# The inverse scale of a weight group on ScalarE, as a product of powers of two

## The chip, the cores and the metric

The kernel runs on one core of a Trainium2 chip. The core has a matmul engine (TensorE, here PE, with its weight loads as PEld), VectorE (DVE), ScalarE (ACT), GpSimd (POOL) and SyncE (SP), and 16 DMA engines. Each engine runs its own list of instructions strictly in order and waits for the others by semaphores. The metric is the device time of one execution in microseconds; of several executions the median is given.

## The reference

A trunk of two layers on 512 tokens of 2048 features. Each layer normalises its input, multiplies it by one wide matrix `w_in`, and feeds three branches: a gated short convolution, a stick-breaking attention of 8 heads, and a gated linear attention (GLA) of 4 heads in chunks of 64 tokens. Each branch output is multiplied by a SiLU gate; the three are concatenated, multiplied by `w_out`, and added to the input.

```
h = _rmsnorm(x, norm_g)
proj = h @ w_in                       # 2048 -> 7696 columns, split into 13 parts
y_conv = _short_conv(cv_h, cv_b, cv_c, conv_w, conv_b) * silu(cv_g)
y_sb   = _stick_breaking(rms(q), rms(k), v) * silu(sb_g)
g      = log_sigmoid(gl_lr @ gla_w_up + gla_b_up) / 16
y_gla  = rms(_gla(gl_q, gl_k, gl_v, g)) * silu(gl_g)
return x + concat(y_conv, y_sb, y_gla) @ w_out
```

All of it is float32.

## The kernel before

**Float32 products from float16 halves.** Each operand of the wide products is split into a high and a low float16 half, and three matmuls (high by high, low by high, high by low) make one product. For that the values must lie in float16's range, so every weight group is multiplied by a power of two, and its result by the inverse power.

**Weight groups.** The two matrices are read in 76 groups of 256 columns, 38 for each layer (30 of `w_in`, 8 of `w_out`). While group i is multiplied, group i+2 is fetched (`fetch`, line 360: DMAs issued by POOL) and group i+1 is prepared. The preparation is hung into the matmul stream of group i by two hooks:

- `squares` (line 379, with 384 for a narrow extra part): ACT squares the whole group and sums each row. The output is thrown away (`junk`), the sums stay.
- `parts_of`: first `wscale`, then the splits. In `wscale` POOL adds the sums over the partitions (line 395), DVE adds the two halves into `m` (398), cuts its exponent out and halves it by integer operations (407: the result is the bit pattern of a number built from half the exponent), makes the scale `ws` from it (411: a constant minus the pattern) and the inverse scale `wu` (413: the pattern plus an offset held in a column, `inoff` for `w_in`, `outoff` for `w_out`). All of these are columns of 128x1. Then ACT makes the high half `wh` (450, 452 for the narrow part, 500) and DVE the low half `wl` (457, 459, 501).

`ws` is needed at once, by `wh` and `wl`. `wu` is read much later, when the group's products leave PSUM.

Some groups are *quick*: they are multiplied by a scheme of seven half-size products in place of eight, and need sums of quarters of the weights (lines 520 to 525) and sums of quarters of the tokens, which `sums_of` makes once for each layer (DVE line 719, with halves by ACT line 727; their tiles are `zw`, `g`, `s`). Quick products leave PSUM through ACT (793, 797) and DVE (794 and the lines behind it).

**What sets the order.** Nearly all instructions are put in order by a scheduler at build time, which runs a timeline of its own for each engine. The start is an exception: from line 107 to the `byhand.__exit__` line DVE and ACT keep among themselves the order in which the code is written. That written order ends with group 1's preparation and the last token copies: `wmax(1, 1)`, `wscale(1)`, `xhigh(3, 0)`, `xhigh(3, 1)`, `whi(1, 0)`, and so on. `xhigh` is an ACT copy of transposed tokens out of PSUM (577, out of psz_72 and psz_73 there), `xlow` the DVE subtraction that belongs to it (584). The token sums (719, 727) are not in the hand-ordered part, so the scheduler may put them in between.

**Then, in each layer,** come the GLA projections (828: two groups by token, the second with 16 extra columns), the other projections (686 to 688 plain, 778 and 781 quick), the GLA stage itself (1023 to 1150) woven into them, the attention in 128-query blocks, and the output projection. Line 1036 and 1133 are GLA's matmuls; 1121 makes the low half of its intra-chunk weights on DVE, and 1120 the high half on ACT.

Names in the order rows and the profile: `x_19` and `x_20` are the high and low tokens, `psp`, `psz` and `psm` are PSUM banks, `wh_74`, `wl_75`, `wh_76`, `wl_77` the two halves of group 1, `wh_110` to `wl_113` those of group 2. The profile leaves the numbers out. Lines from 414 on have a number lower by 1 in the changed kernel, from 1166 on lower by 2.

## Time and profile before

| | |
|---|---|
| median of 3 runs | 1655.18 us (1652.79 to 1658.44) |
| profiled execution, its own time | 1652.11 us |
| its span | 1650.3 us |
| PE busy | 1621.0 us (98%) |
| DVE busy | 1415.1 us (86%), 2377 instructions |
| ACT busy | 1185.3 us (72%), 1743 instructions |
| POOL busy | 270.0 us (16%) |

A row of a group of instructions reads: line, engine, operation, output and inputs with their shapes, count, then the busy time of all and the mean of one in ns, then the engine's idle time just before them and what ended it. A row of the timeline reads: start, length, engine, line, operation, and in brackets the idle time before it and the instruction that released it. The length of an instruction overlaps the start of the next on its engine; the distance of two starts is called its pitch here. A row of waits gives engine, tile and line that waited, the instruction that it waited for, the total in us, how often, and the longest.

### The profile page before, as it was taken

How to read it: one execution, taken by the hardware profiler on the slowest of the kernel's cores; microseconds unless marked ns; L12 is line 12 of the kernel's file. 1: busy time of each engine (PE TensorE's matmuls, PEld its weight loads, DVE VectorE, ACT ScalarE, POOL GpSimd, SP SyncE). 2: the span in 40 equal slices, each digit the busy share in tenths (PEclk: the TensorE clock that was granted, in tenths of full speed). 3: DMA queues.
4: the chain of work that ended last, by engine and by line, in shares of the span. 5: the costliest groups of instructions: out<-in, count | busy, mean ns of one | idle time of the engine just before them, and what ended most of it. 6: DMA issues, size and time to landing. Idle time of an engine off the chain costs nothing.

```text
span 1650.3 us, 41607 instructions
## 1 busy us (share of the span) xinstructions
PE 1621.0 (98%) x17914; PEld 1341.0 (81%) x17914; DVE 1415.1 (86%) x2377; ACT 1185.3 (72%) x1743; POOL 270.0 (16%) x298
## 2 busy tenths in 40 slices
PE   7999999999999999999999999999999999999999
PEld 5746668988999968789986467689898989668998
DVE  7977989969797979798689689898898989888893
ACT  8667787857777776756765687788786868666571
POOL 0121121111212121111112112112121212111110
PEclk9999999999999999999999999999999999999999
DMA  7144344496767686644543442635777766683441
GB/s 260 58 150 122 70 133 86 111 159 148 167 148 167 148 167 175 170 157 149 193 141 104 115 116 66 178 78 151 148 163 150 161 155 150 158 229 129 154 155 53
DMA packets 193913, 234.90 MB, mean 142 GB/s; under 512 B 90226, under 2 KB 154044, under 8 KB 193216
## 3 DMA queue, kind: packets, MB, share of 16 engines
q0 software_dynamic: 76992, 177.22, 39.9%
q1 hardware_dynamic: 107728, 45.56, 13.7%
q10 hardware_dynamic: 9008, 9.45, 1.8%
q8 instruction: 140, 2.29, 0.6%
q14 instruction: 45, 0.37, 0.1%
HBM read 179.65 MB, written 14.68 MB: 118 GB/s over the span
## 4 chain that ended last, share of the span: by engine, by line
PE 40%; DVE 5%; ACT 3%; DMA 1%; issue 1%; POOL 0%; DVEq 0%; ACTq 0%; POOLq 0%
PE psp L781 11%; PE psp L778 7%; PE psp L828 5%; PE psp L697 3%; PE psp L698 3%; PE psp L699 3%; PE psp L686 3%; PE psp L687 3%; PE psp L688 2%; DVE wl L501 1%; ACT junk L379 1%; ACT wh L500 1%; DVE za L1265 1%; PE psm L1289 1%; DMA st<-in_w_in_dram 1%
## 5 line engine op out<-in xcount | busy, mean ns | idle before, releaser
L500 ACT ACTIVATE wh<-st,ws 128x1024 f16<-128x1024 f32 x252 | 281.7, 1147 | 194.0 <-DVE st L520 96.7
L501 DVE SCALAR_TENSOR_TENSOR wl<-st,ws,wh 128x1024 f16<-128x1024 f32 x252 | 318.0, 1283 | 37.9 <-ACT wh L500 37.8
L379 ACT ACTIVATE junk<-st 128x2048 uint8<-128x2048 f32 x150 | 285.7, 1905 | 16.7 <-DMA st<-in_w_in_dram 8.5
L778 PE MATMUL psp<-s,wh 128*128 128x256 f16 x1152 | 195.6, 273 | 0.0
L778 PEld LDWEIGHTS <-wh 128*128 128x128 f16 x1728 | 168.3, 98 | 22.4 <-issue 2.1
L781 PE MATMUL psp<-wh,s 128*128 128x128 f16 x2048 | 176.7, 219 | 0.0
L697 PE MATMUL psp<-wh,m 128*128 128x256 f16 x640 | 174.5, 273 | 0.0
L698 PE MATMUL psp<-wl,m 128*128 128x256 f16 x640 | 174.5, 273 | 0.0
L699 PE MATMUL psp<-wh,m 128*128 128x256 f16 x640 | 174.5, 273 | 0.0
L781 PE MATMUL psp<-wl,s 128*128 128x128 f16 x1024 | 173.2, 219 | 0.0
L781 PEld LDWEIGHTS <-s 128*128 128x128 f16 x3072 | 172.9, 98 | 0.0
L457 DVE SCALAR_TENSOR_TENSOR wl<-st,ws,wh 128x2048 f16<-128x2048 f32 x68 | 158.9, 2347 | 14.7 <-ACT wh L450 14.7
L450 ACT ACTIVATE wh<-st,ws 128x2048 f16<-128x2048 f32 x66 | 130.7, 1998 | 41.8 <-DVE ws L411 22.8
L360 POOL DMA_DIRECT2D st<-in_w_in_dram x114 | 102.7, 905 | 344.3 <-DVE w7l L501 119.9
L778 PE MATMUL psp<-s,wl 128*128 128x256 f16 x576 | 156.7, 273 | 0.0
L395 POOL PARTITION_ALL_REDUCE wgm<-wm x75 | 54.3, 724 | 489.9 <-ACT junk L379 477.2
L781 PEld LDWEIGHTS <-m 128*128 128x128 f16 x2304 | 131.1, 98 | 2.2 <-issue 1.6
L382 POOL DMA_DIRECT2D st<-st x34 | 53.8, 1584 | 276.5 <-ACT junk L379 236.1
L778 PEld LDWEIGHTS <-wl 128*128 128x128 f16 x864 | 84.5, 98 | 16.0 <-issue 6.0
L781 PE MATMUL psp<-wh,m 128*128 128x128 f16 x1024 | 91.5, 219 | 0.3 <-DVE raw L794 0.3
L781 PE MATMUL psp<-wl,m 128*128 128x128 f16 x512 | 87.5, 219 | 0.0
L688 PEld LDWEIGHTS <-wl 128*128 128x128 f16 x448 | 43.8, 98 | 53.7 <-DVE wl L457 2.3
(442 smaller groups left out, 4203.0 us busy)
## 6 DMA issues: line engine op xcount, KB each, us to landing
st<-in_w_in_dram POOLq DMA_DIRECT2D x114, 1024.0 KB, 8.2
st<-in_w_out_dram POOLq DMA_DIRECT2D x32, 1024.0 KB, 8.4
st<-st POOLq DMA_DIRECT2D x34, 512.0 KB, 7.0
st<-in_w_in_dram SPq DMA_DIRECT2D x6, 1024.0 KB, 11.8
mixd<-g POOLq DMA_DIRECT2D x20, 256.0 KB, 6.9
x<-in_x_dram SPq DMA_DIRECT2D x4, 1024.0 KB, 5.1
qT<-in_x_dram ACTq DMA_DIRECT2D x8, 512.0 KB, 6.2
qT<-xs ACTq DMA_DIRECT2D x8, 512.0 KB, 3.9
```

What stands on the lines that cost most here:

```text
L360: queue.dma_start(s_, src[l, h * HK * P:(h + 1) * HK * P, c0:c0 + GW].rearrange("(k p) n -> p k n", p=P), max_dma_last_dim=1024)
L379: sq = S.activation(junk(HK * GW).rearrange("p (k n) -> p k n", k=part.shape[1]), part, AF.Square, accum_out=peak[i][:, h:h + 1])
L450: hi = S.activation(wh[:, :, :GW], staged[i][h], AF.Copy, scale=scales[i])
L457: V.scalar_tensor_tensor(wl[:, :, :GW], staged[i][h], scales[i], wh[:, :, :GW], ALU.mult, ALU.subtract)
L500: hi = S.activation(h_, b, AF.Copy, scale=sc)
L501: V.scalar_tensor_tensor(l_, b, sc, h_, ALU.mult, ALU.subtract)
L697: T.matmul(o, ah[:, t, k, :], wh[:, kk, :n], start=st_, stop=False, skip_group_check=True)
L698: T.matmul(o, ah[:, t, k, :], wl[:, kk, :n], start=False, stop=False, skip_group_check=True)
L699: return T.matmul(o, al[:, t, k, :], wh[:, kk, :n], start=False, stop=en, skip_group_check=True)
L778: mm = T.matmul(o, w[q_][:, kk, :], a[p_][:, :, kk, :], start=st_, stop=en, skip_group_check=True)
L781: mm = T.matmul(o[:, t * P:(t + 1) * P], a[p_][:, t, kk, :], w[q_][:, kk, :], start=st_, stop=en, skip_group_check=True)
L828: mm = T.matmul(o[:, :n], a_[:, t, k, :], w[k // HK][part][:, k % HK, :n], start=i == 0 and k == 0, stop=i == 2 and k == KT - 1)
```

## The change

The inverse scale `wu` of a group is no longer made by DVE from bit patterns. ACT makes it as a float product: it copies the pattern of line 407, read as a float (a power of two), and multiplies it by a column that now holds a power of two in place of an exponent offset. The columns `inoff` and `outoff` are products in place of integer sums, as many as before. The sum on line 398 takes its second operand as a column and gets a lower bound of 2^-120, so that the product has a normal number to work on.

```
-        V.tensor_scalar(inoff[lift], xun.bitcast(I32), float((50 + lift - 127) << 23), None, ALU.add)
+        V.tensor_scalar(inoff[lift], xun, 2.0 ** (50 + lift), None, ALU.mult)
...
-            first = V.tensor_tensor(m, gm[:, 0:1], gm[:, 1:2], ALU.add)
+            first = V.tensor_scalar(m, gm[:, 0:1], gm[:, 1:2], 2.0 ** -120, ALU.add, ALU.max)
...
         u = sm(1, "wu", bufs=6)
-        V.tensor_scalar(u.bitcast(I32), m.bitcast(I32), (outoff[l] if src is w_out else inoff)[lift][:, l:l + 1],
-                        None, ALU.add)
+        S.activation(u, m, AF.Copy, scale=(outoff[l] if src is w_out else inoff)[lift][:, l:l + 1])
...
-                V.tensor_scalar(outoff[l][lift][:, l:l + 1], pmx[:, 0:1].bitcast(I32), float((50 + lift - 127) << 23),
-                                None, ALU.add)
+                V.tensor_scalar(outoff[l][lift][:, l:l + 1], pmx[:, 0:1], 2.0 ** (50 + lift), None, ALU.mult)
```

The scheduler weighs the new instructions, so other instructions change places too. Three places follow. The first is ACT at the end of the hand-ordered part, where group 1 is prepared. Before:

```order
L384 ACTIVATE junk_67_359,wm_64_350<-kT_17_176 128x256
L577 ACTIVATE x_19_185<-psz_72_371 128x1024
L577 ACTIVATE x_19_185<-psz_73_381 128x1024
L727 ACTIVATE s_179_1275<-zw_181_1277 128x1024
L450 ACTIVATE wh_74_391<-st_16_173,ws_70_367 128x8x256
L452 ACTIVATE wh_74_391<-kT_17_176,ws_70_367 128x8x16
L917 ACTIVATE v_79_407<-psp_85_515 128x256
L379 ACTIVATE junk_104_684,wm_103_683<-st_82_410 128x2048
L450 ACTIVATE wh_76_399<-st_16_173,ws_70_367 128x8x256
L452 ACTIVATE wh_76_399<-kT_17_176,ws_70_367 128x8x16
```

The same place in the changed kernel:

```order
L384 ACTIVATE junk_67_359,wm_64_350<-kT_17_176 128x256
L726 ACTIVATE s_179_1275<-zw_181_1277 128x1024
L413 ACTIVATE wu_71_369<-wq_68_361,inoff0_156 128x1
L576 ACTIVATE x_19_185<-psz_72_371 128x1024
L576 ACTIVATE x_19_185<-psz_73_381 128x1024
L449 ACTIVATE wh_74_391<-st_16_173,ws_70_367 128x8x256
L451 ACTIVATE wh_74_391<-kT_17_176,ws_70_367 128x8x16
L916 ACTIVATE v_79_407<-psp_85_515 128x256
L726 ACTIVATE s_179_1275<-zw_182_1278 128x1024
L379 ACTIVATE junk_104_684,wm_103_683<-st_82_410 128x2048
L449 ACTIVATE wh_76_399<-st_16_173,ws_70_367 128x8x256
L451 ACTIVATE wh_76_399<-kT_17_176,ws_70_367 128x8x16
```

The new ACTIVATE stands ahead of the two token copies, as `wscale(1)` is written ahead of `xhigh(3, 0)`; the first token half (727, now 726) moved ahead of it, and a second one ahead of wh_76. On DVE the sum zw_181 that 726 reads has L302 and a copy L311 ahead of it, which stood behind it or later.

The second place is DVE where group 2's first low half, wl_111, is made. Before:

```order
L719 TENSOR_TENSOR s_179_1275<-zw_184_1296,s_179_1275 128x1024
L719 TENSOR_TENSOR zw_185_1297<-zw_185_1297,x_20_186 128x1024
L947 CAST qT_100_677<-lr_114_754 128x48
L947 CAST qT_100_677<-lr_116_813 128x48
L457 SCALAR_TENSOR_TENSOR wl_111_745<-st_82_410,ws_108_740,wh_110_744 128x8x256
L719 TENSOR_TENSOR g_186_1298<-zw_185_1297,g_186_1298 128x1024
L719 TENSOR_TENSOR zw_184_1296<-x_19_185,zw_185_1297 128x1024
```

And now:

```order
L718 TENSOR_TENSOR zw_185_1297<-zw_185_1297,x_20_186 128x1024
L948 TENSOR_TENSOR lr_114_754<-lr_114_754,qT_100_677 128x16
L948 TENSOR_TENSOR lr_116_813<-lr_116_813,qT_100_677 128x16
L917 SCALAR_TENSOR_TENSOR v_80_408<-psp_117_821,v_80_408 128x256
L718 TENSOR_TENSOR g_186_1298<-zw_185_1297,g_186_1298 128x1024
L718 TENSOR_TENSOR zw_184_1296<-x_19_185,zw_185_1297 128x1024
L946 CAST qT_100_677<-lr_114_754 128x48
L946 CAST qT_100_677<-lr_116_813 128x48
L456 SCALAR_TENSOR_TENSOR wl_111_745<-st_82_410,ws_108_740,wh_110_744 128x8x256
```

The sums g_186 and zw_184 moved from behind wl_111 to ahead of it.

The third place is DVE in layer 0's GLA stage, near the point where zw_319, a quick product, leaves PSUM. Before:

```order
L398 TENSOR_TENSOR wq_326_2745<-wgm_327_2746 128x1
L1110 SCALAR_TENSOR_TENSOR th_134_989<-zw_236_1718,th_134_989 128x256 x3
L407 TENSOR_SCALAR wq_326_2745<-wq_326_2745 128x1
L501 SCALAR_TENSOR_TENSOR w7l_314_2576<-st_216_1489,ws_305_2565,w7h_313_2575 128x1024
L411 TENSOR_SCALAR ws_328_2750<-wq_326_2745 128x1
L413 TENSOR_SCALAR wu_329_2752<-wq_326_2745,inoff1_158 128x1
L794 TENSOR_TENSOR zw_319_2685<-psp_321_2689,zw_319_2685 128x256
L1121 SCALAR_TENSOR_TENSOR za_256_2020<-psz_259_2023,za_256_2020 128x512
L1121 SCALAR_TENSOR_TENSOR e_258_2022<-psz_260_2042,e_258_2022 128x512
```

And now:

```order
L398 TENSOR_SCALAR wq_326_2745<-wgm_327_2746 128x1
L1109 SCALAR_TENSOR_TENSOR th_134_989<-zw_236_1718,th_134_989 128x256 x3
L1120 SCALAR_TENSOR_TENSOR za_256_2020<-psz_259_2023,za_256_2020 128x512
L407 TENSOR_SCALAR wq_326_2745<-wq_326_2745 128x1
L1120 SCALAR_TENSOR_TENSOR e_258_2022<-psz_260_2042,e_258_2022 128x512
L500 SCALAR_TENSOR_TENSOR w7l_314_2576<-st_216_1489,ws_305_2565,w7h_313_2575 128x1024
L793 TENSOR_TENSOR zw_319_2685<-psp_321_2689,zw_319_2685 128x256
L411 TENSOR_SCALAR ws_328_2750<-wq_326_2745 128x1
```

Two of GLA's low halves moved ahead of w7l and of zw_319, and L411 behind it; L413 is gone.

## The prediction

> **What bounds the kernel now.** I read the page's busy times first, then the engines by stretch, then what TensorE waited for.

> ```profile
> span 1650.3 us, 41607 instructions
> PE 1621.0 (98%) x17914; PEld 1341.0 (81%) x17914; DVE 1415.1 (86%) x2377; ACT 1185.3 (72%) x1743; POOL 270.0 (16%) x298
> ```

> TensorE (PE) is busy for 1621.0 of 1650.3 us, so 29.3 us is all that any edit beside the matmuls can win. The stretches show where those lie; after each start and end come the length and the busy time of PE, PEld, DVE, ACT and POOL.

> ```profile
> 0.00:41.30 41.30, 32.42 (x216) 24.20 (x217) 32.88 (x88) 33.67 (x46) 3.58 (x9) 0.96 0.78 260
> 41.30:82.50 41.20, 38.61 (x302) 29.29 (x300) 41.20 (x69) 27.04 (x32) 6.55 (x6) 1.00 0.20 58
> 82.50:165.00 82.50, 82.50 (x554) 45.87 (x553) 60.88 (x141) 57.03 (x72) 15.88 (x19) 1.00 0.47 136
> 165.00:206.30 41.30, 39.10 (x375) 26.66 (x374) 39.50 (x74) 32.97 (x58) 6.01 (x4) 1.00 0.32 70
> 330.00:412.00 82.00, 76.19 (x965) 70.12 (x963) 67.14 (x110) 56.02 (x91) 12.63 (x13) 1.00 0.82 155
> 1609.00:1650.30 41.30, 37.73 (x493) 35.29 (x490) 14.52 (x25) 7.70 (x8) 0.40 (x1) 0.99 0.17 53
> ```

> PE idles 8.9 us at the start, 2.6 at 41 to 82, none at 82 to 165, 2.2 at 165 to 206, 5.8 at 330 to 412 (where the DMA share is 0.82) and 3.6 in the tail, 23.1 together; the other 6.2 us lie in small pieces. Where PE never idles, work on VectorE (DVE) and ScalarE (ACT) is hidden. DVE is full (41.20 of 41.20) only at 41 to 82, so there its order decides. These are PE's waits that the edit could touch:

> ```profile
> PE psp L778 <- DVE zw L794: 3.9, 2, 2.0
> PE psp L828 <- ACT wh L441: 2.5, 1, 2.5
> PE psp L778 <- DVE w7l L501: 2.1, 2, 1.1
> PE psp L778 <- DVE g L794: 1.6, 1, 1.6
> PE psp L688 <- DVE wl L457: 1.3, 1, 1.3
> PE psp L828 <- ACT wh L450: 1.1, 1, 1.1
> PE psp L781 <- DVE raw L794: 1.0, 2, 0.7
> ```

> **The change, part by part. The tiny instructions.** These groups show those it touches, and the nearest to those it adds.

> ```profile
> L413 DVE TENSOR_SCALAR wu<-wq,inoff 128x1 int32<-128x1 int32 x60 | 12.4, 207 | 0.0
> L413 DVE TENSOR_SCALAR wu<-wq,outoff 128x1 int32<-128x1 int32 x16 | 3.3, 205 | 0.0
> L398 DVE TENSOR_TENSOR wq<-wgm 128x1 f32<-128x1 f32 x75 | 11.8, 157 | 24.7 <-POOL wgm L395 24.2
> L1343 DVE TENSOR_SCALAR gb<-wu 128x1 f32<-128x1 f32 x16 | 3.4, 213 | 0.0
> L205 ACT ACTIVATE xr<-xr 128x1 f32<-128x1 f32 x8 | 1.6, 203 | 0.2
> L202 ACT ACTIVATE xr<-ssq,epst 128x1 f32<-128x1 f32 x4 | 1.2, 289 | 0.1
> ```

> DVE loses 76 additions, 12.4 + 3.3 = 15.7 us. The 75 sums L398 turn from two tensors into a tensor with a column operand; L1343 is such an instruction, so each grows by about 213 - 157 = 56 ns, 4.2 us. DVE gains 11.5 us by duration. ACT gets 76 ACTIVATEs of 128x1: no row shows one with a column as scale, so it lies between L205 (203 ns, no column) and L202 (289 ns, a column as bias). I take L202, as the operand kind decides: 76 x 0.289 = 22 us, at least 15.4. Where ACT has slack neither figure is time: it is busy for 57.03 of 82.50 us where PE never idles. The six tiny instructions that make the offsets only change operation; I cost them at nothing, and the most they could lose is their number by 0.21 us, 1.2 us.

> [...]

> **The hand-ordered start.** In the first group the new ACTIVATE stands right ahead of the first wh on ACT, and PE waits for that wh 2.5 us (L828 <- ACT wh L441). Between 0.1 us (nothing but overlap) and 0.29 is added: I take **+0.2 us**.

> **The second group, 40 to 75 us: the largest term.** `wscale` of group 1 stands in the hand-written order ahead of the last two token copies (L577, psz_72 and psz_73). Before, ACT had nothing of `wscale` to do; now the inverse scale is on ACT, must wait for DVE's L407, and both copies and wh_74 stand behind it. ACT, DVE and PE now:

> ```profile
> 39.91 1.96 ACT L577 ACTIVATE x<-psz 128x1024 f16<-128x1024 f32 x2
> 43.42 1.06 ACT L727 ACTIVATE s<-zw 128x1024 f16<-128x1024 f32 x1 [1.55 <-DVE zw L719]
> 44.75 2.00 ACT L450 ACTIVATE wh<-st,ws 128x2048 f16<-128x2048 f32 x1 [0.27 <-DVE ws L411]
> 51.00 0.39 ACT L452 ACTIVATE wh<-kT,ws 128x128 f16<-128x128 f32 x1
> ...
> 42.17 1.22 DVE L719 TENSOR_TENSOR zw<-zw,x 128x1024 f32<-128x1024 f32 x1
> 43.30 0.15 DVE L407 TENSOR_SCALAR wq<-wq 128x1 int32<-128x1 int32 x1
> 44.63 0.20 DVE L413 TENSOR_SCALAR wu<-wq,inoff 128x1 int32<-128x1 int32 x1
> 44.75 1.21 DVE L584 TENSOR_TENSOR x<-psz,x 128x1024 f16<-128x1024 f32 x1
> 72.49 2.33 DVE L457 SCALAR_TENSOR_TENSOR wl<-st,ws,wh 128x2048 f16<-128x2048 f32 x1
> 74.75 1.20 DVE L719 TENSOR_TENSOR g<-zw,g 128x1024 f32<-128x1024 f32 x1
> 75.88 1.21 DVE L719 TENSOR_TENSOR zw<-x,zw 128x1024 f32<-128x1024 f16 x1
> ...
> 51.44 2.94 PE L828 MATMUL psp<-wh,x 128*128 128x272 f16 x24 [0.64 <-ACT wh L452]
> 74.88 0.39 PE L688 MATMUL psp<-x,wl 128*128 128x512 f16 x1 [1.31 <-DVE wl L457]
> ```

> The copies, 39.91 to 41.87, filled a hole ahead of L727, which waited for DVE. In the new order ACT waits for that sum first. It comes at about 43.9, since L302 and a copy L311 now stand ahead of it on DVE (before, the sum ran 42.17 to 43.39, so about 0.6 later). Then L727 to 45.1, the new ACTIVATE 0.2, two copies 1.96, and wh_74 starts at 47.3 instead of 44.75: 2.5 us late. wh_76 moves back further, since a second L727 is now ahead of it: its narrow part ends near 54.8 instead of 51.4, and PE resumes near 54.9 instead of 51.44, 3.5 us late. Later PE waited for DVE anyway: wl_111 began at 72.49, then came two sums, 74.75 and 75.88. In the new order these two are ahead of wl_111, 2 x 1.13 us, and DVE lost about 0.3 us more near 41, so wl_111 starts near 75.0 and PE gets it 2.5 us later than at 74.88. The two delays don't add: PE, 3.5 us late, gives 1.0 back out of its old wait of 1.31. Behind it PE has no idle time until 165 (82.50 of 82.50), so nothing there absorbs it: **+2.5 us**. Its bounds are 0 (the sums come earlier than this replay has them) and 3.5.

> **GLA stages.** PE waits twice for L794, 3.9 us. The first place is this:

> ```profile
> 193.81 1.28 DVE L501 SCALAR_TENSOR_TENSOR w7l<-st,ws,w7h 128x1024 f16<-128x1024 f32 x1
> 195.19 0.42 DVE L794 TENSOR_TENSOR zw<-psp,zw 128x256 f32<-128x256 f32 x1
> 195.52 0.68 DVE L1121 SCALAR_TENSOR_TENSOR za<-psz,za 128x512 f16<-128x512 f32 x1
> ...
> 195.66 0.27 PE L778 MATMUL psp<-x,wh 128*128 128x256 f16 x1 [2.03 <-DVE zw L794]
> ```

> In the new order L411 and L413 (0.06 + 0.12 us of pitch) no longer stand ahead of L794, but two L1121 of 0.60 us do, one of them ahead of w7l. PE, for its part, has 19 matmuls of the intra-chunk product and a pass over w7h and w7l ahead of the point where it waits, so it now waits for w7l, ready near 196.3; it fills about 1.2 us of the 2.8 us after 193.5 with work. 2.03 turns into about 1.6: **-0.4 us** (bounds -2.0, if PE arrives late from the first stretch and DVE doesn't, and +1.2, if both L1121 show). The twin in layer 1 has only one L1121 in place of L413, 0.60 for 0.12, and the old wait stays: **+0.5 us** (0 to 0.6).

> **Everywhere else** u stands mostly right ahead of its wh on ACT, where at the end of layer 0 PE waits 1.1 us for wh L450: **+0.1 us** (0.1 to 0.29). DVE's list is shorter by 0.12 us of pitch for each group (44.63 to 44.75 in the rows above) and longer by about 0.05 for L398. At the eight places where PE waits for DVE (3.9 + 2.1 + 1.6 + 1.3 + 1.0 = 9.9 us in the list) that is worth 8 x 0.07: **-0.5 us** (0 to -9.9, if all these waits went). Sum: 0.2 + 2.5 - 0.4 + 0.5 + 0.1 - 0.5 = **+2.4 us**. The profiled execution was 1652.11 us (span 1650.3 and 1.8 around it), so 1654.5; the median of the three runs lies 3.07 above it, so the forecast for the median is **1657.6 us**.

> **The rivals.** *Relief (faster).* DVE releases most of PE's waits, and it loses 76 x 0.12 = 9.1 us of pitch (44.63 to 44.75) and gains 75 x about 0.05 = 3.8: if the 5.3 us net reaches PE, the time is 1649.9. Against it: those waits lie at eight places, and only one or two tiny instructions stand ahead of each.

> *ACT's queue blocks (slower).* The mechanism of the second group repeats: an ACTIVATE that needs L407 stands at the head of an in-order queue, and DVE puts sums of 1.13 us between L398, L407 and L411. In layer 0's reshuffled GLA stretch some eleven such ACTIVATEs have other ACT work between them and their wh, which PE or DVE is fed by. It decides if PE has no lead over that work: six places that pass on 1.1 us make 6.6, on top of +2.4, so 1664.2. For it: DVE ended most waits of ACT, and wl then waits for wh.

> ```profile
> ACT wh L450 <- DVE ws L411: 22.8, 15, 5.3
> DVE wl L501 <- ACT wh L500: 37.8, 40, 5.4
> ```

> Against it: those 37.8 us cost PE next to nothing today, since hardly any wait of PE's list ends with them.

> *The slower engine for a small product (slower).* If each inverse scale were on the path, the difference of L202's 289 ns and L413's 207 would count 76 times, 6.2 us: 1661.4. [...] Against it: the list of PE's waits holds none that ends with L413, and where PE never idles ACT has 25 us of slack.

> *Nothing.* The delay at 75 is made up where PE waits for other things (the 5.8 us at 330 to 412 are largely transfers, DMA share 0.82, which would start no later), and 1655.2 stays. That the change doesn't do what it says I give no chance: the instruction order shows 76 ACTIVATEs in L413's place.

> **How the numbers follow.** About 0.3% (5.0 us) is what a measurement of this kernel can tell from no change. Forecast 0.55, nothing 0.18, blocked queue 0.17, slower engine 0.03, relief 0.07. The first two lie within 0.3% of 1655.18, the next two above 1660.1; relief at 1649.9 is just below 1650.2. So faster 0.07, same 0.73, slower 0.20. The range takes in half of the blocked case and stops short of the relief: 1652.0 to 1663.0. Forecast's own: 1655 to 1660.

> **What would show it.** L413 moves to ACT, 76 rows of 0.2 to 0.3 us; L398 near 0.21. In the stretch 41 to 82 PE idles about 5 us instead of 2.6, wh L452 released late near 54.8, wl_111 started near 75.0. PE's idle time at 165 to 206 falls from 2.2 to about 1.8, and at 82 to 165 it stays at zero. If PE idles newly at 82 to 165 or 206 to 330 behind ACT's wh, the queue blocks; if the waits for L794 and L501 vanish, it is relief. The forecast is wrong if 41 to 82 is unchanged.

## The result, and the profile after

The change is slower, and outside the range. Its median over four executions is 1670.31 us (1664.62 to 1679.99), against 1653.99 us (1648.19 to 1658.44) for four of the kernel before timed with it: a ratio of 1.0117, with a 95% interval from 1.0090 to 1.0144. The forecast was 1657.6 us and the range ended at 1663.0.

The unaltered change was timed twice more, beside the experiments. *again* had a median of 1667.16 us against 1651.12 (1.0114, 1.0083 to 1.0146), *again2* 1664.06 against 1653.09 (1.0063, 1.0039 to 1.0087). The lowest of all 14 executions is 1660.69 us, so every one is slower than the forecast, and they spread over 19 us. A steady loss and a loss that varies from execution to execution have to be told apart.

The page of the changed kernel (profiled execution 1679.99 us) begins so:

```profile
span 1678.2 us, 41610 instructions
PE 1631.6 (97%) x17914; PEld 1344.1 (80%) x17914; DVE 1410.7 (84%) x2301; ACT 1198.3 (71%) x1819; POOL 263.7 (16%) x298
```

DVE lost 76 instructions and ACT gained 76, as foreseen. PE has as many matmuls as before, but is busy for 10.6 us more: it ran at a lower clock in places (0.95 to 0.98 in three of the stretches below, 1.00 in the same stretches before). And it idles for 46.6 us instead of 29.3. The durations were right. These rows give, by line, the shortest, median and longest instruction in ns:

```profile
L413 ACT ACTIVATE wu<-wq,inoff x60: 278/294/351, 16.7 to 1477.3; 128x1 f32<-128x1 f32 x60
L413 ACT ACTIVATE wu<-wq,outoff x16: 278/294/297, 681.0 to 1642.4; 128x1 f32<-128x1 f32 x16
L398 DVE TENSOR_SCALAR wq<-wgm x75: 192/209/226, 42.9 to 1641.0; 128x1 f32<-128x1 f32 x75
```

The prediction had 289 ns for the first two and 213 for the third. So the price of the instructions is not where the time went. These are the stretches of the changed kernel, with the columns of the prediction's (after the five engines come the granted clock, the DMA share and GB/s):

```profile
0.00:41.30 41.30, 31.66 (x211) 23.62 (x212) 32.67 (x85) 32.64 (x45) 3.11 (x9) 0.96 0.78 260
41.30:82.50 41.20, 37.67 (x293) 28.82 (x292) 40.92 (x65) 28.84 (x35) 5.58 (x7) 0.96 0.17 54
82.50:165.00 82.50, 82.50 (x513) 45.56 (x511) 58.78 (x134) 53.20 (x72) 16.18 (x19) 1.00 0.44 130
206.30:330.00 123.70, 122.33 (x1398) 98.41 (x1396) 113.59 (x197) 100.01 (x154) 21.71 (x24) 1.00 0.43 114
330.00:412.00 82.00, 77.26 (x953) 70.29 (x951) 66.91 (x113) 56.72 (x100) 14.04 (x15) 0.98 0.79 148
1500.00:1600.00 100.00, 94.61 (x1003) 82.91 (x1002) 82.15 (x94) 60.94 (x64) 9.81 (x13) 0.95 0.46 149
```

At 41 to 82 PE now idles 3.5 us and the clock is 0.96; at 82 to 165 it idles not at all, as before. New are 1.4 us at 206 to 330 and 5.4 us at 1500 to 1600, where the clock falls to 0.95 as well; the kernel before idled at neither:

```profile
206.30:330.00 123.70, 123.70 (x1456) 101.26 (x1454) 116.03 (x211) 101.35 (x161) 23.79 (x26) 1.00 0.43 110
1500.00:1600.00 100.00, 100.00 (x1351) 94.74 (x1350) 87.42 (x101) 61.09 (x61) 11.64 (x15) 1.00 0.44 145
```

**Where the lag arises.** Every kernel here issues 16272 projection matmuls (tile `psp`). In short stretches neighbouring ones change places (at most 304 of them carry other tile names than in the kernel before, in the kernels of the table); everywhere else they come in the same order. So, away from these stretches, the start of the n-th can be compared between two traces; the difference is the lag behind the profiled execution of the kernel before. In us, at some places of the time before (the experiments in the right columns are explained below):

| time before | change | again | again2 | mix_other_queue | late_one | late_old2 |
|---|---|---|---|---|---|---|
| 41 | +0.8 | +1.3 | +1.4 | +1.8 | +1.1 | +1.4 |
| 150 | +3.0 | +3.6 | +3.6 | +4.0 | +1.0 | +1.2 |
| 210 | +2.4 | +2.9 | +3.0 | +3.3 | +2.7 | +0.8 |
| 350 | +4.7 | +5.2 | +5.3 | +5.6 | +2.9 | +0.9 |
| 380 | +4.6 | +5.5 | +5.3 | +0.3 | +3.0 | -4.9 |
| 900 | +8.6 | +6.2 | +6.1 | +1.8 | +3.7 | -2.5 |
| 1000 | +9.8 | +7.4 | +7.1 | +2.8 | +4.6 | -1.6 |
| 1150 | +12.1 | +8.1 | +7.7 | +3.4 | +6.9 | -1.8 |
| 1210 | +18.2 | +7.9 | +13.6 | +4.3 | +12.1 | -1.6 |
| 1480 | +18.8 | +8.2 | +14.5 | +4.5 | +12.0 | -0.5 |
| 1640 | +27.9 | +18.0 | +14.5 | +5.6 | +12.0 | -0.5 |

Three stretches hold the large jumps: 350 to 380 and 1150 to 1210, where the attention of a layer begins, and 1480 to 1500, where its last mixed outputs are loaded. A jump can be there in one execution of the changed kernel and missing in the next, and the kernel before had one itself at 350 to 380. *mix_other_queue* has the same change (one load moved to another queue), did not have that jump, and so gains 5.3 us there. Outside these stretches the three unaltered executions lose 12.8, 8.1 and 8.6 us and *mix_other_queue* 8.9 (the first one's 12.8 hold a slow load near 690, 3.0 us, and a stretch of half clock near 1020, 1.4 us; the second trace of that version, *mix_again*, loses 12.0, with 2 us between 1210 and 1480 that the others lack). That is the steady part, 8 to 9 us, and the prediction gave it 2.4. Of it 0.8 to 1.8 us are there at 41 us already. *null_swap* below, which leaves the inverse scale on DVE, has 1.0 us there too, so most of that is likely an early start of the one execution of the kernel before, and about 7 us are left behind 41 us. The rest, 15.1, 9.9, 5.9 and -3.3 us, is the varying part.

### The profile page after: what moved, and what is told of

The parts are those of the page before. It is cut to its first block, busy times and chain, and to the rows that moved or that the text cites. A ratio compares the mean times of both kernels' runs of the same rounds, so it can differ in the third digit from the quotient of the medians.

```text
span 1678.2 us, 41610 instructions
## 1 busy us (share of the span) xinstructions
PE 1631.6 (97%) x17914; PEld 1344.1 (80%) x17914; DVE 1410.7 (84%) x2301; ACT 1198.3 (71%) x1819; POOL 263.7 (16%) x298
## 3 DMA queue, kind: packets, MB, share of 16 engines
q8 instruction: 140, 2.29, 0.6%
## 4 chain that ended last, share of the span: by engine, by line
PE 21%; DVE 13%; ACT 8%; DMA 5%; issue 3%; POOL 0%; SPq 0%; DVEq 0%; ACTq 0%; POOLq 0%
PE psp L780 5%; PE psp L827 3%; DVE wl L500 2%; PE psp L698 2%; PE psp L696 2%; PE psp L697 2%; ACT junk L379 2%; ACT wh L499 2%; PE psp L777 2%; PE psp L685 2%; PE psp L686 2%; PE psp L687 1%; DMA m<-mixd 1%; DMA st<-in_w_in_dram 1%; DMA st<-st 1%
## 5 line engine op out<-in xcount | busy, mean ns | idle before, releaser
L500 DVE SCALAR_TENSOR_TENSOR wl<-st,ws,wh 128x1024 f16<-128x1024 f32 x252 | 317.5, 1280 | 46.2 <-ACT wh L499 46.1
L449 ACT ACTIVATE wh<-st,ws 128x2048 f16<-128x2048 f32 x66 | 130.6, 1994 | 30.7 <-PE psp L686 13.0
L395 POOL PARTITION_ALL_REDUCE wgm<-wm x75 | 48.6, 648 | 520.7 <-ACT junk L379 505.5
```

What stands on the lines that cost most here:

```text
L449: hi = S.activation(wh[:, :, :GW], staged[i][h], AF.Copy, scale=scales[i])
L500: V.scalar_tensor_tensor(l_, b, sc, h_, ALU.mult, ALU.subtract)
```

## The experiments

**The change once more: again.** No edit.

> The changed kernel unaltered, for a second trace. If its loss belongs to its order (ScalarE's queue in the second group, and waits for transfers late in each layer), the waits for the copied tokens near 44 us (about 2.6 us) and for the rescaled mix near 685 and 1507 us (2.5 and 5.1 us) come again and the ratio stays near 1.012. If the long transfers of the first trace (20 us to landing instead of 10) were a disturbance of that one execution, the waits near 1183 and 1507 us shrink to under 1 us, the granted clock is near 0.998, and the ratio falls to 1.006 to 1.008.

**And once more: again2.** No edit.

> The changed kernel once more, for more executions beside the three below on one chip. If slow transfers strike at random in some executions, its times fall in groups: about 1658 without any, about 1663 with one of 5 us, 1668 to 1680 with the late mix. If they belonged to this order, all would lie at 1664 and above, as the eight so far did.

Measured: 1.0114 and 1.0063, as above. What follows: the first timing was no accident, and the lags up to 350 agree within 0.6 us in all three. Of the waits that *again* was to show, those near 44 us (2.59) and near 1507 us (3.96 and 1.19) came again; the one near 685 did not. The six executions of *again2* fall into two groups 5 us apart, 1660.7 to 1661.9 and 1666.2 to 1666.9, as the expectation has it for transfers that are slow in some executions, but none comes near its 1658. What differs comes mostly from two of the three stretches, 1150 to 1210 (+6.1, -0.2, +5.9 us) and behind 1480 (+9.1, +9.8, 0.0).

**The second group's ACTIVATE moved behind the copies: late_one.** The change, but the ACTIVATE of group 1 alone is issued behind the two copies and behind `wh_74`.

```diff
-        S.activation(u, m, AF.Copy, scale=(outoff[l] if src is w_out else inoff)[lift][:, l:l + 1])
+        late[i] = (u, m, (outoff[l] if src is w_out else inoff)[lift][:, l:l + 1])
+        if i != 1:
+            unscale(i)
...
+    def unscale(i):
+        u, m, off = late.pop(i)
+        S.activation(u, m, AF.Copy, scale=off)
...
     whi(1, 0)
+    unscale(1)
```

> The change with one instruction moved: group 1's inverse scale is made behind the last two token copies and the first high half, not ahead of them. By ScalarE's queue the wait near 44 us (2.6 us) and the stretch of half clock near 48 us (3.4 us at half speed, 1.7 us) go, so it is 3 to 5 us faster than the change: a ratio 0.002 to 0.003 lower. If the second group is made up for later, or the loss lies elsewhere, it stays where the change is.

The timeline of the changed kernel shows what it is to undo (start, length, engine, line):

```profile
44.57 1.06 ACT L726 ACTIVATE s<-zw 128x1024 f16<-128x1024 f32 x1 [3.96 <-DVE zw L718]
45.53 0.28 ACT L413 ACTIVATE wu<-wq,inoff 128x1 f32<-128x1 f32 x1
45.72 1.92 ACT L576 ACTIVATE x<-psz 128x1024 f16<-128x1024 f32 x2
46.78 2.52 PE L827 MATMUL psp<-wh,x 128*128 128x256 f16 x16 [2.58 <-ACT x L576]
47.53 2.00 ACT L449 ACTIVATE wh<-st,ws 128x2048 f16<-128x2048 f32 x1
75.47 2.33 DVE L456 SCALAR_TENSOR_TENSOR wl<-st,ws,wh 128x2048 f16<-128x2048 f32 x1
77.86 0.39 PE L687 MATMUL psp<-x,wl 128*128 128x512 f16 x1 [0.58 <-DVE wl L456]
```

ACT stands idle for 3.96 us, then come the sum's half, the new ACTIVATE and the two copies, and PE waits 2.58 us for the first of the copies. In *late_one* (its lines 837, 465 and 697 are 827, 456 and 687 of the change) the same places read:

```profile
44.37 1.91 PE L837 MATMUL psp<-wh,x 128*128 128x256 f16 x16
47.38 2.24 PE L837 MATMUL psp<-wh,x 128*128 128x256 f16 x16 [1.10 <-DVE zun L191]
73.54 2.33 DVE L465 SCALAR_TENSOR_TENSOR wl<-st,ws,wh 128x2048 f16<-128x2048 f32 x1
75.92 0.39 PE L697 MATMUL psp<-x,wl 128*128 128x512 f16 x1 [1.66 <-DVE wl L465]
```

The wait of 2.58 us is gone, `wl_111` starts 1.93 us earlier, and PE has it at 75.92 instead of 77.86. From 41 to 150 us the lag of the change grows by 2.2 us, that of *late_one* not at all (1.1 and 1.0). The median is 1664.10 us, 3.06 below *again* on the same chip; its ratio of 1.0082 (1.0048 to 1.0115) overlaps the one of *again*, so the trace shows this step and the timing alone would not. What follows: the mechanism that the prediction gave the second group is there and worth 2.2 us, but it is only a part: *late_one* is still slower than the kernel before. Behind 150 us the two can't be compared step by step, since the scheduler gave *late_one* another order in layer 0's GLA stage too: there it has a wait of 2.29 us at 197, with half clock behind it (granted clock 0.96 from 165 to 206, 1.00 in the change), and none at 222 where the change has one.

**The halves alone: only_sum, old_sum.** *only_sum* is the kernel before with the new L398, *old_sum* the change with the old one.

```diff
-            first = V.tensor_tensor(m, gm[:, 0:1], gm[:, 1:2], ALU.add)
+            first = V.tensor_scalar(m, gm[:, 0:1], gm[:, 1:2], 2.0 ** -120, ALU.add, ALU.max)
```

> The kernel before with one of the changes alone: the sum of a group's two halves takes a column operand and a lower bound; the inverse scale stays an integer addition on VectorE. If the loss is ScalarE's queue (the new instruction ahead of the two token copies), this is within 0.2% of the kernel before. If the loss comes from the scheduler's reordering, which this edit sets off as well, it is as slow as the change, 1.008 to 1.014.

> The change with the old sum (two tensors, no lower bound), the inverse scale on ScalarE. If ScalarE's queue is the cause, as slow as the change, 1.008 to 1.014, and the second group waits about 2.6 us for the copied tokens. If the reordering by the longer sum is the cause, within 0.3% of the kernel before.

Measured: *only_sum* 1655.34 us, 1.0041 (1.0021 to 1.0060); *old_sum* 1650.89 us, 1.0016 (0.9992 to 1.0041). With the inverse scale on ACT and the old sum the time cannot be told from before in the median, though two of its ten executions took 1666 and 1668 us against 1649 to 1656 of the others. *old_sum* still waits 2.53 us for the copies near 47 us, so that wait does not make the change as slow as it is. By the middle of the intervals the smaller half, a sum longer by some 50 ns, costs more than the half that gives the change its name; the two intervals overlap, so this order of the two is not shown. Neither expectation of *only_sum* came: it is slower than before by more than 0.2%, and by half as much as the reordering alone was to cost. The middles of the two halves add up to 0.57%: near the lower one of the three results for the whole, and below the intervals of the other two.

**Two edits that change next to nothing: null_swap, dve_twice.** *null_swap* is the kernel before with the lines that make `ws` and `wu` exchanged. *dve_twice* is the kernel before with line 413 standing twice, so that DVE has 76 more of just the instructions that the change takes from it (the second overwrites the first with the same value).

```diff
-        sc = sm(1, "ws")
-        V.tensor_scalar(sc.bitcast(I32), m.bitcast(I32), -1.0, float((204 - lift) << 23), ALU.mult, ALU.add)
         u = sm(1, "wu", bufs=6)
         V.tensor_scalar(u.bitcast(I32), m.bitcast(I32), (outoff[l] if src is w_out else inoff)[lift][:, l:l + 1],
                         None, ALU.add)
+        sc = sm(1, "ws")
+        V.tensor_scalar(sc.bitcast(I32), m.bitcast(I32), -1.0, float((204 - lift) << 23), ALU.mult, ALU.add)
```

```diff
         V.tensor_scalar(u.bitcast(I32), m.bitcast(I32), (outoff[l] if src is w_out else inoff)[lift][:, l:l + 1],
                         None, ALU.add)
+        V.tensor_scalar(u.bitcast(I32), m.bitcast(I32), (outoff[l] if src is w_out else inoff)[lift][:, l:l + 1],
+                        None, ALU.add)
```

> The kernel before with the inverse scale emitted ahead of the scale on VectorE: the same 76 + 76 instructions, the wide scale 0.12 us later. If small changes of order cost what the change costs, this may lie anywhere between 0.997 and 1.010. If only real work counts, it is within 0.3% of the kernel before.

> The kernel before with the removed cost doubled: VectorE makes each inverse scale twice, 76 more instructions of 0.12 us, 9 us of VectorE. If VectorE's small instructions are on the path, 5 to 9 us slower, 1.003 to 1.006. If they are hidden and only order counts, the same as the kernel with the longer sum alone, whose order it nearly shares, 1.002 to 1.006 through the same places, or the same as before.

Measured: 1654.07 us, 1.0009 (0.9993 to 1.0025), and 1654.53 us, 1.0009 (0.9994 to 1.0025). What follows: 76 more instructions on DVE, 76 x 0.12 = 9.1 us of pitch, with the order that came with them, cost at most 0.25%, and 0.09% by the middle. That is a net figure: the trace of *dve_twice* gains 5.1 us of lag at 350 to 380, where its transfers lie apart (below), and loses elsewhere. In *null_swap* the scale `ws`, where nothing but the exchanged line stands between, starts 0.31 us behind line 407 in place of 0.18. That is more than the 0.05 us that the longer sum adds ahead of it, and the time stays within 0.25% of before. Together they speak against the length of the tiny instructions, taken away or added, as the source of a per cent. And not every new order costs: these two moved instructions too.

**Both at once: late_old, late_old2.** The old sum and the late ACTIVATE of group 1 together; the inverse scales stay on ACT. *late_old2* is the same kernel timed again on another chip, with the change beside it.

> Both edits that helped alone, together: the inverse scale on ScalarE with the old sum, and group 1's inverse scale behind the last token copies. If the second group's 3 us were not made up for in the kernel with the old sum, this is about 3 us faster than that one, 1648 us, a ratio of 0.998 to 0.999 to the kernel before. If every order stands for itself and gains don't add, anything from 1.000 to 1.008.

> The best version so far again, to tell its 0.16% from nothing: 0.997 to 0.9995 if it is really faster by the 3 us that the second group no longer loses and the 5 us that the transfers at the start of layer 0's attention cost the kernel before; 1.000 or more if the first result was luck.

Measured: 1648.71 us, 0.9984 (0.9967 to 1.0001), then 1648.62 us, 0.9975 (0.9958 to 0.9992). The second interval is below one: in that timing this version beats both kernels, the one before by a quarter of a per cent (the first interval just includes one). In its text it differs from the change in one DVE operand form and in the place of one ACTIVATE of 0.28 us, and the time differs by 15 us (1664.06 against 1648.62 on the same chip). What follows: the inverse scale on ACT costs nothing by itself. What costs is, as far as these runs go, the order that the whole program got with it. No run has the longer sum in an otherwise unchanged order; that its 50 ns are not the cause rests on *null_swap* and *dve_twice*.

One piece of that order can be seen where the attention of layer 0 begins. There `qT` is made by DMA transposes from SP's queue, while POOL fetches weights. In the kernel before:

```profile
333.25 9.73 SPq L1366 DMA_TRANSPOSE qT<-qp  x2
335.25 1.77 POOL L360 DMA_DIRECT2D st<-in_w_in_dram  x2 [3.91 <-DVE wl L457]
```

and in the view of the DMA issues of 325 to 362 us (KB each, median us to landing):

```profile
st<-in_w_in_dram POOLq DMA_DIRECT2D x4, 1024.0 KB, 12.4
st<-st POOLq DMA_DIRECT2D x1, 512.0 KB, 17.6
```

The same two views of *late_old2*, and its stretch of 330 to 412:

```profile
332.05 6.72 SPq L1374 DMA_TRANSPOSE qT<-qp  x2
338.86 1.76 POOL L360 DMA_DIRECT2D st<-in_w_in_dram  x2 [5.87 <-DVE wl L465]
```

```profile
st<-in_w_in_dram POOLq DMA_DIRECT2D x4, 1024.0 KB, 8.5
st<-st POOLq DMA_DIRECT2D x2, 512.0 KB, 8.3
330.00:412.00 82.00, 81.33 (x1068) 75.85 (x1066) 72.66 (x120) 63.95 (x113) 14.34 (x17) 1.00 0.72 155
```

Before, the fetch is issued 2.0 us behind the transposes, while they run; the fetches land after 12.4 us and the transposes take 9.73. In *late_old2* the fetch comes 6.8 us behind, when the transposes are done, the fetches land after 8.5, and PE idles 0.7 us in a stretch where it idled 5.8. The change has the distance of before:

```profile
337.94 9.78 SPq L1364 DMA_TRANSPOSE qT<-qp  x2
339.82 1.77 POOL L360 DMA_DIRECT2D st<-in_w_in_dram  x2 [3.92 <-DVE wl L456]
```

Eight profiled executions (before, *null_swap*, *late_one*, the change three times, and twice with the other queue for the mixed loads, below) have the fetch 1.9 to 2.1 us behind the transposes in both layers. Those are 16 places, and at 10 of them PE waited for `kT<-raw`, 2.6 us on average, with further waits behind. In the six others (*only_sum*, *old_sum*, *dve_twice* and the three with both edits) no weight fetch is issued while the transposes run, and of their 12 places one has such a wait, of 0.4 us. This association is shown; it was not tried by moving the transposes and nothing else. And the place of the fetch alone does not decide it. With the wait the two transposes of `qT` took 9.73 us (layer 0 before), 9.78 and 8.94 (both layers of the change), 9.31 (layer 0 of *again*) and 7.75 (layer 1 of *again2*). Without it, at the same distance, they took 5.46 in layer 1 of the kernel before and 4.94 in layer 0 of *mix_other_queue*, no longer than where they lie apart (6.72 in *late_old2*, 7.01 in *only_sum*). *mix_other_queue* in layer 0:

```profile
338.87 4.94 SPq L1364 DMA_TRANSPOSE qT<-qp  x2
340.75 1.77 POOL L360 DMA_DIRECT2D st<-in_w_in_dram  x2 [3.92 <-DVE wl L456]
```

The change itself had both in layer 1: the wait at first (transposes of 8.94 us) and in *again2* (7.75), and none in *again*. So, as far as these traces go, the order makes the loss possible, and something that no run here shows decides in which execution it comes. A loss that comes in some executions fits the spread: the kernel before took 1644.6 to 1664.6 us in 29 executions, *late_old2* 1647.2 to 1654.2 in twelve beside them (*late_old* had one of twelve at 1663.7).

**The mixed loads: mix_other_queue, mix_again, late_old_mix.** In the profiled executions of the change and of *again* PE waits near 1500 us for `m`, the mixed outputs that are loaded back for the output projection. DMA view, DVE and PE of the change:

```profile
m<-mixd SPq DMA_DIRECT2D x2, 256.0 KB, 20.6
1510.65 0.49 DVE L1172 TENSOR_SCALAR m<-m,ratio 128x1024 f16<-128x1024 f16 x1 [5.82 <-DMA m<-mixd]
1511.20 0.40 PE L698 MATMUL psp<-wh,m 128*128 128x256 f16 x1 [3.90 <-DVE m L1172]
```

Before, the same loads landed after 9.4 us:

```profile
m<-mixd SPq DMA_DIRECT2D x2, 256.0 KB, 9.4
```

The edit lets one half of these loads be issued by ACT's queue instead of SP's: on the change (*mix_other_queue*, and *mix_again* on another chip) and on the best version (*late_old_mix*).

```diff
-    order(nc.sync.dma_start(mix[i][:, :, ks, :], mixd[l]...), lastmm[0])
+    order((nc.scalar if i else nc.sync).dma_start(mix[i][:, :, ks, :], mixd[l]...), lastmm[0])
```

> The change, with the low half of the stored branch outputs fetched by ScalarE's DMA queue rather than SyncE's, where it stands behind the transposes. If PE's wait near 1500 us is this transfer, queued behind slow transposes, the wait for the rescaled mix (5.2 us and half clock after it, 10 us together) goes and the kernel is 4 to 10 us faster than the change, 1657 to 1663 us, with no execution over 1668. If all transfers are slow there whatever their queue, the wait stays at 4 us or more and the time at 1664 to 1680.

> The change with the low half of the stored branch outputs fetched by ScalarE's DMA queue, again, for more executions than four. If that transfer behind slow transposes is what makes the change's slowest executions, the median stays 4 to 8 us below the change's on this chip and no more than one in ten lies above 1668. If the four were luck, the median is within 2 us of the change's.

> The best version so far (old sum, group 1's inverse scale behind the copies) with the low half fetched by the other queue as well. If the queue takes away an execution like its 1663.68 and nothing else, the median stays at 1648 to 1650 and the highest under 1656. If ScalarE pays for issuing three transfers a layer, 1 to 2 us slower.

Measured: *mix_other_queue* 1662.53 us over four executions, 1.0076 (1.0049 to 1.0103); *mix_again* 1661.86 us over twelve, 1.0051 (1.0032 to 1.0070), 2.2 us below *again2* beside it, with intervals that overlap; *late_old_mix* 1651.42 us, 0.9982 (0.9963 to 1.0001), 2.8 us above *late_old2* beside it, with a highest execution of 1658.11: neither the median nor the highest that the expectation gave for the queue as the cause. The profiled execution of *mix_other_queue* had no wait near 1500. That of *mix_again* had one again, for another transfer:

```profile
PE psm L1287 <- DMA th<-za: 7.1, 2, 6.4
```

Inconclusive: of the 4 to 8 us expected of *mix_again* 2.2 came, two of its twelve executions lay above 1668, and SP's queue is not shown to be the cause. The late transfers strike some executions of several kernels (*old_sum* lost 16 us here in its profiled execution, *late_one* nothing with nearly the order of the change). Why some and not others stays open.

## Why the prediction was wrong

**The prices were right and did not matter.** 294 ns and 209 ns stood against 289 and 213. The forecast was argued correctly that far: the work on ACT is hidden, as *old_sum* and *late_old2* show.

**The second group: right mechanism, size nearly right.** The prediction had PE get `wl_111` 2.5 us late; it was 77.86 - 74.88 = 2.98 us in the first trace, but 0.8 of that was there at 41 us, ahead of the group. From 41 to 150 us the lag grows by 2.2 us in all four traces of the change's order in the table, +2.5 was forecast. `wl_111` started at 75.47 where 75.0 was forecast. The way there differed: PE waited at the copies themselves (2.58 us), not for `wh_76`. That wait had a consequence that no row of before announces. In *again*, this is the time right after it, with the clock as the third number from the end:

```profile
47.50:50.70 3.20, 3.20 (x16) 2.28 (x15) 3.20 (x7) 3.20 (x5) 0.00 (x0) 0.50 0.01 3
```

The granted clock is 0.50 there, in the trace of the change for 3.41 us (48.02 to 51.43). That costs 1.7 us of matmul time, but here not on top: PE arrived later at `wl_111`, and its old wait of 1.31 us shrank to 0.58, since DVE set the moment. PE's idle time at 41 to 82 rose to 3.5 us and not to the 5 of the prediction's sign, since part of the delay is slower matmuls and not idle time.

**The start: +0.2 not resolvable.** PE's wait for the first `wh` was 2.7 us in the change, but 1.3 in *again*, 1.6 in *again2* and 2.4 in *mix_other_queue*, against 2.5 before. It varies by more than the term.

**GLA, layer 0: the number was near, the wait was another, and the next wait was missed.** From 150 to 210 the lag falls by 0.6 to 0.8 us in all four; -0.4 was forecast. But PE does not wait for `w7l` there, as the replay had it. The scheduler moved GLA's own matmuls ahead on PE, and these wait 0.79 us for the second of the two low halves:

```profile
198.05 0.83 PE L1132 MATMUL psz<-th,v 128*128 128x128 f16 x12 [0.79 <-DVE e L1120]
```

So the nearness of the number is partly luck. (The replay also says that one of the two low halves stands ahead of `w7l`; in the order rows both do, and its 196.3 us for `w7l` counts both. `w7l` ended at 199.2 in a trace that was some 3 us late.) Then the lag rises by 2.3 us up to 350, in all four alike. Most of it, 1.5 us, is one place, some 25 us behind the one that the prediction replayed:

```profile
220.12 0.68 DVE L1147 TENSOR_TENSOR e<-e,e 128x512 f32<-128x512 f32 x1
220.72 1.00 DVE L1196 TENSOR_SCALAR kT<-zw,par 128x512 f32<-128x512 f32 x2
221.63 0.42 DVE L793 TENSOR_TENSOR qT<-psp,qT 128x256 f32<-128x256 f32 x1
222.10 0.27 PE L777 MATMUL psp<-x,wh 128*128 128x256 f16 x1 [1.37 <-DVE qT L793]
```

The kernel before, with lines higher by 1 or 2:

```profile
211.98 1.00 DVE L1198 TENSOR_SCALAR kT<-zw,par 128x512 f32<-128x512 f32 x2
216.14 0.42 DVE L794 TENSOR_TENSOR qT<-psp,qT 128x256 f32<-128x256 f32 x1
217.97 0.69 DVE L1148 TENSOR_TENSOR e<-e,e 128x512 f32<-128x512 f32 x1
```

DVE now does L1196 (once far ahead) and L1147 (once behind) right before the L793 that PE waits for, and PE has a wait of 1.37 us where it had none. So the stretch where "PE never idles" in the profile of before got a new bound by order alone.

**GLA, layer 1: +0.5 exactly, and again not all.** From 1000 to 1012 the lag rises by 0.5 us in *again*, *again2* and *mix_other_queue*. In the first trace it rises by 1.9, with a stretch of half clock behind the wait (0.50 for 3.41 us from 1020.82; why only there is not shown). But from 900 to 1000 all four lose 1.0 to 1.2 us that no term covered, and from 380 to 900 another 0.7 to 1.5 (4.1 in the first trace, where a slow load of `m` near 690 adds 3.0).

**The end of layer 0: +0.1.** The wait for `wh` L449 grew from 1.1 to 1.7 us, the lag rose by 0.6 at 822, and at 845 it was given back.

**Relief, -0.5: not seen.** No stretch shows it, and *dve_twice* points the same way: 9.1 us of DVE pitch more, with its order, cost 0.09%.

**The step that failed is "everywhere else".** The sum was made of the places that were looked at, and every other place was taken to keep its order but for 0.12 us of pitch. The places that were replayed came out near the forecast: 2.2, -0.6, 0.5 and 0.0 us behind 41 us, 2.1 together, where 2.7 was forecast. But the whole program was reordered, and the terms that nobody replayed (+2.3, +1.2, +0.7 us and more) came to about 5 us of the steady 7, where -0.5 was forecast. Also wrong was the clause, in the rival "nothing", that the transfers at 330 to 412 "would start no later" and were therefore no part of the matter: late transfers there, at 1150 to 1210 and near 1500 make the varying part, 5 to 10 us at a time. That the profiled execution of before held one such loss itself made its 5.8 us of idle time there look like a property of the kernel.

**The rivals.** "ACT's queue blocks" gave 1664.2 us, which is what *again2* measured, but not by its mechanism: PE's new waits in the GLA stretches end with DVE (L793) and not with ACT, and the blocked queue shows at one place only, the second group. "The slower engine for a small product" gave 1661.4; it falls with *old_sum* and *late_old2*, which have all 76 products on ACT and take 1.0016 and 0.9975 of the time before. The single instruction is the longer one on ACT, 294 ns against 207, and that decides nothing about the time. "Relief" and "nothing" are refuted by the first interval.

**What stays open.** How much of the steady part belongs to which moved instruction outside the second group and the place at 222; why the transfers are slow in some executions, and how often under each order. 0.3% was taken as what a measurement can tell; three timings of the same changed kernel gave 1.0063, 1.0114 and 1.0117, so with so few executions and a varying part of 10 us it is more.

## What to carry to other kernels

When a scheduler orders the program, a small edit is priced by the order that it leaves behind, not by its instructions: compare the order of every stretch that has no slack on the releasing engine (here DVE ahead of PE's PSUM banks), or widen the range by what a reordering of the same kernel does, here from 0.9975 to 1.0117 among six versions with nearly the same work. Where a list is kept in order by hand, a new instruction that needs a late result belongs behind the work that is ready, not at its place in the text: moving one ACTIVATE of 0.28 us took 2.2 us off the lag. And measure the halves of an edit apart, since a slow one can hide a harmless one.

## What the runs showed of the hardware

What lies ahead of them can be counted in the traces of the kernel before and of the change. The stretches of half clock of one trace start whole steps of 3.413 us apart: in the change at 17.30, 48.02, 365.46, 1020.82 and 1508.93 us, of which the last three lie 93, 285 and 428 steps behind the one at 48.02; in the kernel before at 17.71 and 1649.28 us, 478 steps apart. So PE's idle time can be counted within each step, here with the columns of the stretches above: the change with the step before the half clock and the half clock itself, then the two steps over which the wait in *old_sum* is spread, and the first of the two that hold the 2.26 us in the kernel before.

```profile
44.61:48.02 3.41, 1.24 (x11) 1.01 (x12) 3.41 (x6) 3.41 (x5) 0.00 (x0) 1.00 0.00 0
48.02:51.43 3.41, 3.14 (x16) 1.94 (x14) 3.41 (x7) 3.41 (x5) 0.00 (x0) 0.50 0.01 2
42.39:45.80 3.41, 2.52 (x24) 2.02 (x21) 3.34 (x9) 0.56 (x1) 0.04 (x1) 1.00 0.00 0
45.80:49.21 3.41, 1.76 (x16) 1.40 (x16) 3.41 (x9) 3.41 (x5) 0.00 (x0) 1.00 0.00 0
355.63:359.04 3.41, 1.60 (x15) 1.28 (x14) 0.22 (x1) 0.00 (x0) 0.00 (x0) 1.00 1.30 193
```

PE idled 2.17 us in the step ahead of the half clock, 0.89 and 1.65 us in the two steps of *old_sum*, and 1.81 us in the one of the kernel before. The wait near 1020 of the change fell into one step, 2.36 us of idle time, with half clock behind it. In these two traces, from where the clock is on record (14 us after the start), there are seven steps at full clock with a step of half clock behind them: PE idled for 1.93 to 2.71 us in each. The other 951 steps at full clock have full clock behind them: PE idled for 1.83 us or less in all but one (1.92 us in the kernel before near 1008). So in these traces half clock came behind steps with 1.93 us of idle time or more, over half of a step, and a wait of 2.0 to 2.6 us had that much in one step (the 2.58 us of the change) or was spread over two (the 2.53 us of *old_sum*). What makes it so is not shown. (The ends of matmuls are modelled, so these idle times are only as exact as those.)

**Transposes and a fetch beside each other.** With a weight fetch issued 1.9 to 2.1 us behind two DMA transposes, the four 1024 KB fetches around them landed after a median of 12.4 and 9.6 us in the two layers of the kernel before, 12.5 and 12.1 in those of the change, and 12.2 in layer 0 of *again*; with none issued while the transposes ran, after 8.5 in layer 0 of *late_old2* and 7.8 in that of *only_sum*. The transposes took 7.75 to 9.78 us at the five places above with PE's wait and 5.46 and 4.94 at the two without. The 512 KB transfer `st<-st` behind them landed after 17.6 us (layer 0 before), 17.9 (both layers of the change) and 18.3 (layer 0 of *again*) where PE had the wait, and after 11.8 in layer 1 of the kernel before, where it had none. What makes the difference between such places is not shown.
